# Zero products ahead of the first transposes, root norms by ScalarE, and one written order for VectorE's recurrent work

## The chip, the cores and the metric

The kernel runs on one core of one Trainium2 chip. A core has TensorE (PE in the profile; its weight loads are listed apart as PEld), VectorE (DVE), ScalarE (ACT), GpSimd (POOL) and SyncE (SP, which here only issues DMAs). The metric is the device time of one execution in microseconds, lower is better. The other numbers come from one further execution that the hardware profiler recorded.

## The reference

One layer of a hybrid decoder over 16 meta tokens and 1024 rows of width 1024, all in float32. `h` holds the meta rows and then the rows of `x`:

```python
u = rmsnorm(h, g_pre_mix)
z = u @ w_in                         # 1024 -> q 512 | k 128 | v 128 | xr 512 | yr 512
attn = sliding_window_attention_with_sinks(q, k, v, sinks)     # 8 heads of 64, window 128
xr = causal_depthwise_conv(xr, conv_w, conv_b)                 # 4 taps
hr = rg_lru(xr, ...)                 # gates by two block products, then h_t = a_t h_{t-1} + u_t
rec = gelu(yr) * hr
h = h + rmsnorm(concat(attn, rec) @ w_out, g_post_mix)
f = square(relu(rmsnorm(h, g_pre_ffn) @ w_ff1)) @ w_ff2        # 1024 -> 4096 -> 1024
h = h + rmsnorm(f, g_post_ffn)
```

`rmsnorm(x, g)` divides a row by the root of its mean square plus 1e-6 and multiplies by `g`. The gates use `mult = sqrt(1 - a*a)`.

## The kernel before

Each product is made of three: an operand is split into a high part (rounded to the type fp32r, by a cast) and a low part (what the cast left out), and high x high, high x low and low x high are summed in PSUM (`mm3`, L123; in block 0 `part`, L242, one of the three at a time over all eight slices of the depth, kc = 0 to 7). The high parts of weights and activations are made by ScalarE (L96, L117, L283), the low parts by VectorE (L99, L118, L287).

**Start.** SyncE's queue loads the meta rows, `x` rows 0 and 1 (each `xt[i]` is 128 rows x 1024), the two gain vectors, and then the column blocks of `w_in` for k, v, q and the first block of xr (`rk`, `rv`, `rq`, `rx`) with `xt[2]` to `xt[7]` between and after them. The rows are worked in four blocks (`ALL`, L251): block 0 holds the meta rows, `xt[0]` and `xt[1]`, and each later block two more `xt`. For a block, `norm_rows` (L212) makes the sum of squares on ScalarE (L215), adds EPS and takes the power -0.5 on GpSimd (`rstd_of`, L164: L167 and L173), and scales the rows on VectorE (L221). `transposed` (L289) then transposes them on TensorE (L296) slice by slice into PSUM and splits each slice into `u[kc]` high (ScalarE, L117) and low (VectorE, L118). The banks of PSUM in which the slices land have three tags with two buffers each (`pt`, `o`, `s`), so in block 0 six slices are under way before one must be emptied by both engines. In block 0, `chained` (L276) writes out an order for ScalarE (index 0) and VectorE (index 1): high part of the k weights, eight splits, then the v weights, the norms of `xt[2]` and `xt[3]`, the q weights and the xr weights. Products follow: k and v high, then their low weights, then q, then xr (L416 to L430).

**Middle.** Scores, softmax and attention of head pair j go on while `next_fill` (L674) projects the other column blocks (q, xr and yr) in between. The xr blocks are evicted from PSUM by ScalarE (`new_x`, L400, L404) and convolved by VectorE (`conv`, L618): a first tap with the bias over 1040 columns (L620) and three more (L625).

**Recurrent part.** `gates` (L729) makes two tanh gates for each of four 128-wide channel blocks c. `recur` (L770) takes a root on ScalarE and then, on VectorE, a scaling (L773), a product (L774) and the scan over time (L775). `rec_out` (L777) applies GeLU to one half (512 rows) of block c, multiplies (L781) and splits the result into `at`. In between, the row blocks kc of `w_out` are loaded by SyncE and split (`split_wo`, L794). The output products `out_mm` (L837) of row tile t run over kc = 0 to 7: kc 0 to 3 use the attention, kc 4 to 7 the recurrent blocks c = 0 to 3 together with `w_out` blocks 4 to 7. The first four tiles begin with kc 0 to 3, then take kc 4 and 5, then 6 and 7.

**Order.** Except where `behind` (L106) adds an ordering, which costs no semaphore, each engine's order is fixed when the kernel is built, by a planner that simulates the program. The functions below stand with the line numbers of the profile.

Of the kernel before, what the change touches and what calls it, by code (L numbers as in the profile page):

```python
# [9 lines left out]
F32 = mybir.dt.float32  # L10
F32R = mybir.dt.float32r
AF = mybir.ActivationFunctionType
ALU = mybir.AluOpType
# [24 lines left out]
def hybrid_layer(  # L38
# [42 lines left out]
    def lut(*args, **kwargs):  # L81
        ins = nc.scalar.activation(*args, **kwargs).ins
        if last_lut[0] is not None:
            tc.add_manual_dep(
                ins, last_lut[0],
                mybir.DependencyInfo(
                    mybir.DependencyClass.NoSync, mybir.DependencyReason.DATA
                ),
                reason="lut",
            )  # L90
        last_lut[0] = ins.name
        return ins

    def split(hi, lo, src, eng=None):
        if eng is None:
            nc.scalar.copy(hi, src)  # L96
        else:
            eng.tensor_copy(hi, src)
        low = nc.vector.tensor_tensor(lo, src, f32(hi), op=ALU.subtract).ins  # L99
        mark[0] = low.name  # L100
        return low
# [38 lines left out]
    meta_t = slot("d", [NMETA, D])  # L140
    nc.sync.dma_start(meta_t, meta_tokens)
    xt = []
# [5 lines left out]

    load_x(0)
    load_x(1)  # L150
    g_r = slot("e", [16, P])
    nc.sync.dma_start(g_r[0:8, :], g_pre_mix.rearrange("o (k p) -> (o k) p", p=P))
    nc.sync.dma_start(g_r[8:16, :], g_pre_ffn.rearrange("o (k p) -> (o k) p", p=P))

# [26 lines left out]
    held_back = []  # L181
# [28 lines left out]
    RMS_SC = 1.0 / math.sqrt(D)  # L210

    def norm_rows(src, n, link=False):  # L212
        xn = slot("d", [P, D])
        ssq = small.tile([P, 1], F32, name="ssq", tag="ssq")
        ins = nc.scalar.activation(  # L215
            xn[:n], src, AF.Square, scale=RMS_SC, accum_out=ssq[:n]
        ).ins
        if link:
            chained(0, ins)
        rs = rstd_of([ssq[:n]], n)  # L220
        ins = nc.vector.tensor_scalar(xn[:n], src, rs, None, op0=ALU.mult).ins  # L221
# [39 lines left out]
    vmt = const.tile([P, P], F32, name="vmt")  # L261
    nc.gpsimd.memset(f32(km), 0.0)
# [18 lines left out]
    def high_w(raw, tag="ws"):  # L281
        hi, lo = pair(tag, [P, KC, P])
        chained(0, nc.scalar.copy(hi, raw).ins)  # L283
        return hi, lo

    def low_w(w, raw):
        chained(1, nc.vector.tensor_tensor(w[1], raw, f32(w[0]), op=ALU.subtract).ins)  # L287

    def transposed(b, xn, after=None):  # L289
        t0, n = ALL[b]  # L290
        for kc in range(KC):
            flip[0] += 1
            pt = bank(("pt", "o", "s")[flip[0] % (2 if b == 1 else 3)])
            o = 0
            for s, m in xn:
                ins = nc.tensor.transpose(  # L296
                    pt[:, o : o + m], s[:m, kc * P : (kc + 1) * P], ident[:m, :m]
                )
# [46 lines left out]
    low_w(wx, rx)  # L345
# [51 lines left out]

        return q, sink_q

    def new_x(tag="d"):  # L400
        xr = slot(tag, [P, TT])

        def sink_x(acc, t0, n):
            nc.scalar.copy(xr[:, t0 : t0 + n], acc)  # L404

        return xr, sink_x


    done = [None, None]
    q0, sink_q0 = new_q()  # L410
    xr0, sink_x0 = new_x("c")
    for b in range(4):
        if b:
            transposed(b, xn if b == 1 else normed(b), done[b])
# [200 lines left out]

    xc = [None] * NLRU

    def conv(c, xr, tag="d"):  # L618
        y = slot(tag, [P, TT])
        taps = [nc.vector.tensor_scalar(  # L620
            y, xr, prm[:, c, 3:4], prm[:, c, 4:5], op0=ALU.mult, op1=ALU.add
        ).ins]
        for k in (2, 1, 0):
            s = 3 - k
            taps.append(nc.vector.scalar_tensor_tensor(  # L625
                y[:, s:], xr[:, : TT - s], prm[:, c, k : k + 1], y[:, s:],
                op0=ALU.mult, op1=ALU.add,
            ).ins)
        xc[c] = y
        if c == 2:  # L630
            held_back.extend(taps[4:])

    ys = [None] * NLRU
    begun = {}
# [7 lines left out]

    def fill_x(c):
        def run(w):
            xr, sink = new_x()
            project(w, ALL, sink)
            conv(c, xr, "b" if c == 3 else "d")
        return run

    def fill_y(c):  # L650
# [119 lines left out]
    def recur(c):  # L770
        r, gi, a = rg[c]
        lut(r, r, AF.Sqrt, scale=-0.25)
        nc.vector.scalar_tensor_tensor(r, a, 1.0, r, op0=ALU.add, op1=ALU.mult)  # L773
        nc.vector.tensor_tensor(gi, gi, r, op=ALU.mult)  # L774
        nc.vector.tensor_tensor_scan(r, a, gi, 0.0, op0=ALU.mult, op1=ALU.add)  # L775

    def rec_out(c, half):  # L777
        o = 512 * half
        y, h = ys[c][:, o : o + 512], rg[c][0]
        lut(y, y, AF.Gelu_apprx_tanh)  # L780
        nc.vector.tensor_tensor(y, y, h[:, NMETA + o : NMETA + o + 512], op=ALU.mult)  # L781
        ah, al = at[half][2 + c // 2]
        split(ah[:, c % 2, :], al[:, c % 2, :], y)
# [9 lines left out]

    def split_wo(kc, tag, eng=None):  # L794
        wo[kc] = pair(tag, [P, D])
        split(wo[kc][0], wo[kc][1], wo_raw[kc], eng)

    gate_parts(0)
    gate_parts(1)
# [6 lines left out]
    decay(3)  # L806
    next_fill()
    for c in range(NLRU):
        recur(c)
# [6 lines left out]
    for kc in range(2, 4):  # L816
        split_wo(kc, "a")
    for cp in (2, 3):
        at[0][cp] = pair("b", [P, 2, 512])
    for c in range(NLRU):  # L820
        rec_out(c, 0)
    for kc in range(4, KC):
        load_wo(kc, ("d", "raw")[kc % 2])
        split_wo(kc, "a")
# [589 lines left out]
```

## Time and profile before

| | |
|---|---|
| median of three runs | 959.78 us (958.34 to 960.52) |
| profiled execution, its own time | 961.63 us |
| its span, first to last instruction | 959.9 us (1.7 us lie around it) |
| granted TensorE clock, mean | 0.996 |
| busy: PE, PEld, DVE, ACT, POOL | 940.3, 784.9, 680.1, 495.0, 157.8 us |

In rows of a timeline the first number is the start in us from the span's start, the second the duration, then engine, line, operation, output and inputs, shapes, and the count; in square brackets stands how long the engine had been idle and what ended that. In rows of stretches each engine has its busy time and, in brackets, its instructions. In rows of waits stand the total in us, the number of waits and the longest.

### The profile page before, as it was taken

How to read it: one execution, taken by the hardware profiler on the slowest of the kernel's cores; microseconds unless marked ns; L12 is line 12 of the kernel's file. 1: busy time of each engine (PE TensorE's matmuls, PEld its weight loads, DVE VectorE, ACT ScalarE, POOL GpSimd, SP SyncE). 2: the span in 40 equal slices, each digit the busy share in tenths (PEclk: the TensorE clock that was granted, in tenths of full speed). 3: DMA queues.
4: the chain of work that ended last, by engine and by line, in shares of the span. 5: the costliest groups of instructions: out<-in, count | busy, mean ns of one | idle time of the engine just before them, and what ended most of it. 6: DMA issues, size and time to landing. Idle time of an engine off the chain costs nothing.

```text
span 959.9 us, 12395 instructions
## 1 busy us (share of the span) xinstructions
PE 940.3 (98%) x4654; PEld 784.9 (82%) x4654; DVE 680.1 (71%) x961; ACT 495.0 (52%) x818; POOL 157.8 (16%) x201
## 2 busy tenths in 40 slices
PE   6999999999999999999999999999999999999997
PEld 6999998878788877888888888888878888888886
DVE  5579989878966786665655466576557676779884
ACT  7556676468445464443555575663533344435451
POOL 4015656600021100000111001100111100003020
PEclk9999999999999999999999999999999999999999
DMA  9211101202236457585646557644767866566422
GB/s 286 53 48 42 38 8 34 66 21 90 88 132 219 131 180 237 157 282 175 219 165 209 154 182 231 219 135 132 170 148 186 199 219 197 178 193 156 113 85 88
DMA packets 85627, 140.74 MB, mean 147 GB/s; under 512 B 5784, under 2 KB 48936, under 8 KB 85568
## 3 DMA queue, kind: packets, MB, share of 16 engines
q1 hardware_dynamic: 75104, 108.51, 36.0%
q0 software_dynamic: 9600, 29.36, 11.9%
q10 hardware_dynamic: 864, 2.10, 0.6%
q8 instruction: 36, 0.59, 0.3%
q14 instruction: 23, 0.19, 0.1%
HBM read 115.70 MB, written 23.07 MB: 145 GB/s over the span
## 4 chain that ended last, share of the span: by engine, by line
PE 88%; DVE 6%; issue 2%; ACT 1%; POOL 1%; DMA 1%; DVEq 0%; SPq 0%; ACTq 0%; POOLq 0%
PE ps_acc L125 10%; PE ps_acc L128 10%; PE ps_acc L129 10%; PE ps_pt L129 6%; PE ps_s L129 6%; PE ps_pt L125 6%; PE ps_pt L128 6%; PE ps_s L128 6%; PE ps_s L125 6%; PE ps_o L129 5%; PE ps_o L128 5%; PE ps_o L125 5%; PE ps_o L597 1%; DVE c L775 1%; POOL c L587 1%
## 5 line engine op out<-in xcount | busy, mean ns | idle before, releaser
L96 ACT CAST ws<-raw 128x1024 fp32r<-128x1024 f32 (+1 forms) x70 | 71.7, 1025 | 120.8 <-PE ps_o L128 45.1
L99 DVE TENSOR_TENSOR ws<-raw,ws 128x1024 fp32r<-128x1024 f32 (+1 forms) x71 | 86.2, 1214 | 43.7 <-ACT ws L96 43.6
L125 PE MATMUL ps_acc<-a,ws 128*128 128x256 f32 (+2 forms) x256 | 85.9, 336 | 1.6 <-ACT d L404 1.4
L129 PE MATMUL ps_acc<-a,ws 128*128 128x256 f32 (+2 forms) x256 | 85.1, 333 | 0.0
L128 PE MATMUL ps_acc<-a,ws 128*128 128x256 f32 (+2 forms) x256 | 85.0, 332 | 0.0
L99 DVE TENSOR_TENSOR b<-b,b 128x1024 fp32r<-128x1024 f32 (+2 forms) x48 | 57.6, 1200 | 23.6 <-PE ps_o L128 15.3
L96 ACT CAST ws<-e 128x1024 fp32r<-128x1024 f32 x42 | 43.9, 1045 | 57.3 <-PE ps_o L128 34.7
L96 ACT CAST b<-b 128x1024 fp32r<-128x1024 f32 (+2 forms) x48 | 49.4, 1030 | 41.3 <-DVE b L912 40.5
L99 DVE TENSOR_TENSOR ws<-e,ws 128x1024 fp32r<-128x1024 f32 x42 | 51.4, 1223 | 20.0 <-ACT ws L96 20.0
L587 POOL TENSOR_SCALAR_AFFINE_SELECT c<-c 128x512 fp32r<-128x512 f32 x64 | 56.4, 905 | 26.3 <-ACT c L96 15.5
L173 POOL TENSOR_TENSOR rs<-ms,half_pow 128x1 f32<-128x1 f32 (+1 forms) x29 | 21.3, 740 | 207.6 <-DVE ms L169 206.2
L125 PEld LDWEIGHTS ps_acc<-a,ws 128*128 128x128 f32 x256 | 48.3, 189 | 6.8 <-ACT d L404 1.6
L129 PEld LDWEIGHTS ps_acc<-a,ws 128*128 128x128 f32 x256 | 48.2, 188 | 5.2 <-issue 0.2
L128 PEld LDWEIGHTS ps_acc<-a,ws 128*128 128x128 f32 x256 | 48.2, 188 | 4.5 <-issue 0.4
L128 PE MATMUL ps_acc<-ws,b 128*128 128x512 f32 (+1 forms) x120 | 46.6, 389 | 1.8 <-DVE ws L99 1.8
L129 PE MATMUL ps_acc<-ws,b 128*128 128x512 f32 (+1 forms) x120 | 46.6, 388 | 0.0
L125 PE MATMUL ps_acc<-ws,b 128*128 128x512 f32 (+1 forms) x120 | 46.4, 387 | 0.0
L125 PE MATMUL ps_pt<-ws,b 128*128 128x512 f32 x112 | 44.2, 395 | 0.0
L128 PE MATMUL ps_pt<-ws,b 128*128 128x512 f32 x112 | 44.1, 394 | 0.0
L129 PE MATMUL ps_pt<-ws,b 128*128 128x512 f32 x112 | 43.9, 392 | 0.0
L128 PE MATMUL ps_s<-ws,b 128*128 128x512 f32 x110 | 43.8, 398 | 0.0
L125 PE MATMUL ps_s<-ws,b 128*128 128x512 f32 x110 | 43.7, 397 | 0.0
(417 smaller groups left out, 2712.4 us busy)
## 6 DMA issues: line engine op xcount, KB each, us to landing
raw<-in_w_ff_dram SPq DMA_DIRECT2D x58, 512.0 KB, 4.4
e<-in_w_ff_dram SPq DMA_DIRECT2D x42, 512.0 KB, 4.2
raw<-in_w_in_dram SPq DMA_DIRECT2D x12, 512.0 KB, 5.7
d<-in_w_ff_dram SPq DMA_DIRECT2D x12, 512.0 KB, 4.1
s_dram<-d POOLq DMA_DIRECT2D x12, 512.0 KB, 4.0
e<-in_w_ff_dram POOLq DMA_DIRECT2D x10, 512.0 KB, 5.7
raw<-in_w_ff_dram POOLq DMA_DIRECT2D x10, 512.0 KB, 5.6
c<-in_x_dram SPq DMA_DIRECT2D x8, 512.0 KB, 8.2
```

The source lines that it names most:

```text
L96: nc.scalar.copy(hi, src)
L99: low = nc.vector.tensor_tensor(lo, src, f32(hi), op=ALU.subtract).ins
L125: ins = nc.tensor.matmul(dst, lh, rh, start=start, stop=False, skip_group_check=True).ins
L128: nc.tensor.matmul(dst, lh, rl, start=False, stop=False, skip_group_check=True)
L129: last_mm[0] = nc.tensor.matmul(dst, ll, rh, start=False, stop=stop, skip_group_check=True).ins.name
L173: last_pow[0] = nc.gpsimd.tensor_tensor(rs[:n], ms[:n], half_pow[:n], op=ALU.pow).ins.name
L587: nc.gpsimd.affine_select(out=m[:, :, side, :], in_=f32(m)[:, :, 1, :], pattern=[[0, 4], [-sign, P]], compare_op=op, fill=0.0, base=0, cha ...
L597: nc.tensor.matmul(po[:, :, oc : oc + n], v, m[:, :, pc : pc + n], start=first and k == 0, stop=last and k == 1, skip_group_check=True,)
L775: nc.vector.tensor_tensor_scan(r, a, gi, 0.0, op0=ALU.mult, op1=ALU.add)
```

## The change

Five things, all ahead of the feed-forward part; what is computed stays the same.

1. **Products of zeros.** TensorE multiplies `km`, just set to zero, with itself into a bank that nobody reads: 11 products of 512 columns as soon as `km` is set, 4 more (`waiting`) behind the transpose of `xt[0]`'s slice 4, and one of 256 columns behind the last transpose of each of the eight slices of block 0. That bank is one of the two of tag `acc`.
2. **Norms of block 0** (`norm_first`): ScalarE takes the root of mean square plus EPS itself and VectorE the reciprocal; GpSimd is left out. For `xt[0]` the sum of squares is shared, 576 columns by ScalarE and 448 by VectorE. The scaling of `xt[0]` and `xt[1]` is made in two halves of 512 columns. The first table that ScalarE loads is the root's.
3. **Weights at the start.** The high part of the k weights is cast by VectorE in place of ScalarE; the cast of the q weights moves ahead of the norms of `xt[2]` and `xt[3]`. The gains land in `vmt`, no longer in a buffer of tag `e`.
4. **Convolution of block c = 2:** the first tap is made by ScalarE from PSUM, piece by piece, right after the copy.
5. **Recurrent part:** the pieces of `recur`, `rec_out` and `split_wo` that VectorE runs get one written order (`queue`); GeLU runs once over 1024 columns per block, no longer twice over 512.

```diff
-    g_r = slot("e", [16, P])
+    vmt = const.tile([P, P], F32, name="vmt")
+    g_r = vmt[:16, :]
...
+    eps_t = const.tile([P, 1], F32, name="eps_t")
+    nc.gpsimd.memset(eps_t, EPS)
+    root = small.tile([P, 1], F32, name="root", tag="root")
+    lut(root, half_pow, AF.Sqrt, scale=-1.0)
...
+    ROW_HALVES = (slice(0, 512), slice(512, D))
+    def norm_first(src, n, cut, parts):
+        xn = slot("d", [P, D])
+        ssq = small.tile([P, 1], F32, name="ssq", tag="ssq")
+        nc.scalar.activation(
+            xn[:n, :cut], src[:n, :cut], AF.Square, scale=RMS_SC, accum_out=ssq[:n]
+        )
+        rest = eps_t
+        if cut < D:
+            rest = small.tile([P, 1], F32, name="ms", tag="ms")
+            nc.vector.tensor_tensor_reduce(
+                out=xn[:, cut:], in0=src[:, cut:], in1=src[:, cut:], scale=1.0 / D,
+                scalar=EPS, op0=ALU.mult, op1=ALU.add, accum_out=rest,
+            )
+        root = small.tile([P, 1], F32, name="root", tag="root")
+        lut(root[:n], ssq[:n], AF.Sqrt, bias=rest[:n])
+        rs = small.tile([P, 1], F32, name="rs", tag="rs")
+        nc.vector.reciprocal(rs[:n], root[:n])
+        for c in parts:
+            chained(1, nc.vector.tensor_scalar(
+                xn[:n, c], src[:n, c], rs[:n], None, op0=ALU.mult
+            ).ins)
+        return xn
...
+    idle, still = bank("acc"), km.rearrange("p a b c -> p (a b c)")
+    def idling(n, cols=512, after=None):
+        made = []
+        for _ in range(n):
+            ins = nc.tensor.matmul(
+                idle[:, :cols], still[:, :P], still[:, :cols],
+                start=True, stop=True, skip_group_check=True,
+            ).ins
+            if after:
+                behind(after, ins)
+            made.append(ins)
+        return made
+    idling(11)
+    waiting = idling(4)
...
     def normed(b):
-        rows = [(meta_t, NMETA)] if b == 0 else []
-        rows += [(xt[2 * b], P), (xt[2 * b + 1], P)]
-        return [(norm_rows(s[:m], m), m) for s, m in rows]
+        if b == 0:
+            return [
+                (norm_first(meta_t, NMETA, D, (slice(0, D),)), NMETA),
+                (norm_first(xt[0], P, 576, ROW_HALVES), P),
+                (norm_first(xt[1], P, D, ROW_HALVES), P),
+            ]
+        return [(norm_rows(xt[i], P), P) for i in (2 * b, 2 * b + 1)]
...
+                if b == 0 and o == NMETA and kc == 4:
+                    behind(ins.ins.name, *waiting)
                 o += m
+            if b == 0:
+                idling(1, 256, ins.ins.name)
...
-    wk = high_w(rk, "b")
+    wk = high_w(rk, "b", 1)
     transposed(0, xn)
     low_w(wk, rk)
     wv = high_w(rv, "b")
     low_w(wv, rv)
+    wq = high_w(rq)
     xn = [(norm_rows(xt[i], P, True), P) for i in (2, 3)]
-    wq = high_w(rq)
...
         def sink_x(acc, t0, n):
             nc.scalar.copy(xr[:, t0 : t0 + n], acc)
+            if y is not None:
+                nc.scalar.activation(
+                    y[:, t0 : t0 + n], acc, AF.Identity,
+                    scale=prm[:, c, 3:4], bias=prm[:, c, 4:5],
+                )
...
+    lane = []
+    def queue(ins):
+        if lane:
+            behind(lane[-1].name, ins)
+        lane.append(ins)
...
     for c in range(NLRU):
-        rec_out(c, 0)
-    for kc in range(4, KC):
+        lut(ys[c], ys[c], AF.Gelu_apprx_tanh)
+    queue(input_scale(0))
+    queue(input_gate(0))
+    queue(split_wo(3, "a"))
+    queue(scan(0))
+    for kc in (4, 5):
         load_wo(kc, ("d", "raw")[kc % 2])
-        split_wo(kc, "a")
+    queue(rec_mult(0, 0))
+    queue(input_scale(1))
+    queue(input_gate(1))
+    queue(scan(1))
+    queue(rec_low(0, 0))
+    queue(rec_mult(1, 0))
+    queue(split_wo(4, "a"))
+    queue(rec_low(1, 0))
+    queue(split_wo(5, "a"))
+    queue(input_scale(2))
+    for kc in (6, 7):
+        load_wo(kc, ("d", "raw")[kc % 2])
+    queue(input_gate(2))
+    queue(scan(2))
+    queue(rec_mult(2, 0))
+    queue(input_scale(3))
+    queue(rec_low(2, 0))
+    queue(input_gate(3))
+    queue(scan(3))
+    queue(rec_mult(3, 0))
+    queue(split_wo(6, "a"))
+    queue(rec_low(3, 0))
+    queue(split_wo(7, "a"))
     for cp in (2, 3):
         at[1][cp] = pair("b", [P, 2, 512])
     for c in range(NLRU):
-        rec_out(c, 1)
+        queue(rec_mult(c, 1))
+    for c in range(NLRU):
+        queue(rec_low(c, 1))
```

`input_scale`, `input_gate`, `scan`, `rec_mult` and `rec_low` are the instructions of L773, L774, L775, L781 and of the split at L783, each in a function of its own.

More of the change, by code (lines that the diff above doesn't have):

```diff
@@ L279, in chained, with high_w @@
         last[e] = ins.name
-    def high_w(raw, tag="ws"):
+    def high_w(raw, tag="ws", e=0):
         hi, lo = pair(tag, [P, KC, P])
-        chained(0, nc.scalar.copy(hi, raw).ins)
+        cast = (nc.scalar.copy, nc.vector.tensor_copy)[e]
+        chained(e, cast(hi, raw).ins)
         return hi, lo
@@ L398, in new_q, with new_x @@
         return q, sink_q
-    def new_x(tag="d"):
+    def new_x(tag="d", c=0):
         xr = slot(tag, [P, TT])
+        y = slot("d", [P, TT]) if c == 2 else None
         def sink_x(acc, t0, n):
             nc.scalar.copy(xr[:, t0 : t0 + n], acc)
-        return xr, sink_x
+            if y is not None:
[3 more added lines that the diff above has]
+                )
+        return xr, sink_x, y
     done = [None, None]
     q0, sink_q0 = new_q()
-    xr0, sink_x0 = new_x("c")
+    xr0, sink_x0, _ = new_x("c")
     for b in range(4):
@@ L616, in hybrid_layer, with conv @@
     xc = [None] * NLRU
[L618 to L622, printed above, removed]
+    def conv(c, xr, tag="d", y=None):
+        if y is None:
+            y = slot(tag, [P, TT])
+            nc.vector.tensor_scalar(
+                y, xr, prm[:, c, 3:4], prm[:, c, 4:5], op0=ALU.mult, op1=ALU.add
+            )
         for k in (2, 1, 0):
             s = 3 - k
-            taps.append(nc.vector.scalar_tensor_tensor(
+            nc.vector.scalar_tensor_tensor(
                 y[:, s:], xr[:, : TT - s], prm[:, c, k : k + 1], y[:, s:],
                 op0=ALU.mult, op1=ALU.add,
-            ).ins)
+            )
         xc[c] = y
-        if c == 2:
-            held_back.extend(taps[4:])
     ys = [None] * NLRU
@@ L644, in run @@
         def run(w):
-            xr, sink = new_x()
+            xr, sink, y = new_x(c=c)
             project(w, ALL, sink)
-            conv(c, xr, "b" if c == 3 else "d")
+            conv(c, xr, "b" if c == 3 else "d", y)
         return run
@@ L768, in decay, with root, input_scale, input_gate @@
         lut(v, v, AF.Tanh, scale=m2sp[:, c : c + 1], bias=m2sp[:, c : c + 1])
-    def recur(c):
-        r, gi, a = rg[c]
[L772 to L777, printed above, removed]
+    lane = []
[3 more added lines that the diff above has]
+        lane.append(ins)
+    def root(c):
+        lut(rg[c][0], rg[c][0], AF.Sqrt, scale=-0.25)
+    def input_scale(c):
+        r, gi, a = rg[c]
+        return nc.vector.scalar_tensor_tensor(
+            r, a, 1.0, r, op0=ALU.add, op1=ALU.mult
+        ).ins
+    def input_gate(c):
+        r, gi, a = rg[c]
+        return nc.vector.tensor_tensor(gi, gi, r, op=ALU.mult).ins
+    def scan(c):
+        r, gi, a = rg[c]
+        return nc.vector.tensor_tensor_scan(
+            r, a, gi, 0.0, op0=ALU.mult, op1=ALU.add
+        ).ins
+    def rec_mult(c, half):
         o = 512 * half
         y, h = ys[c][:, o : o + 512], rg[c][0]
-        lut(y, y, AF.Gelu_apprx_tanh)
-        nc.vector.tensor_tensor(y, y, h[:, NMETA + o : NMETA + o + 512], op=ALU.mult)
+        return nc.vector.tensor_tensor(
+            y, y, h[:, NMETA + o : NMETA + o + 512], op=ALU.mult
+        ).ins
+    def rec_low(c, half):
         ah, al = at[half][2 + c // 2]
-        split(ah[:, c % 2, :], al[:, c % 2, :], y)
+        y = ys[c][:, 512 * half : 512 * half + 512]
+        return split(ah[:, c % 2, :], al[:, c % 2, :], y)
     wo_raw = [None] * KC
@@ L795, in split_wo @@
         wo[kc] = pair(tag, [P, D])
-        split(wo[kc][0], wo[kc][1], wo_raw[kc], eng)
+        return split(wo[kc][0], wo[kc][1], wo_raw[kc], eng)
     gate_parts(0)
@@ L808, in hybrid_layer @@
     for c in range(NLRU):
-        recur(c)
+        root(c)
     load_wo(0, "raw")
@@ L815, in hybrid_layer @@
     split_wo(1, "e")
-    for kc in range(2, 4):
-        split_wo(kc, "a")
+    split_wo(2, "a")
     for cp in (2, 3):
```

2 lines of the change are left out of this document (removed).

## The prediction

> **What bounds the kernel now.** First the page's busy times and the chain that ended last, then the stretches, then the list of TensorE's waits.
>
> ```profile
> PE 940.3 (98%) x4654; PEld 784.9 (82%) x4654; DVE 680.1 (71%) x961; ACT 495.0 (52%) x818; POOL 157.8 (16%) x201
> PE 88%; DVE 6%; issue 2%; ACT 1%; POOL 1%; DMA 1%; DVEq 0%; SPq 0%; ACTq 0%; POOLq 0%
> ...
> 5.80:13.50 7.70, 6.04 (x27) 4.94 (x28) 3.94 (x9) 5.88 (x12) 1.78 (x4) 1.00 1.10 316
> 50.00:80.00 30.00, 30.00 (x216) 27.97 (x215) 23.38 (x79) 15.28 (x44) 8.45 (x7) 1.00 0.20 54
> 150.00:176.00 26.00, 24.60 (x183) 23.16 (x182) 22.93 (x55) 17.26 (x48) 17.77 (x16) 1.00 0.13 35
> 245.00:262.00 17.00, 15.99 (x69) 12.40 (x68) 17.00 (x17) 5.33 (x8) 0.00 (x0) 1.00 0.26 82
> ...
> PE ps_s L296 <- DVE d L221: 5.8, 1, 5.8
> PE ps_acc L125 <- ACT d L404: 1.4, 1, 1.4
> PE ps_pt L129 <- DVE b L99: 1.0, 2, 0.5
> ```
>
> TensorE is busy 98% of the span and carries 88% of the chain. What the edited parts can give is therefore only what TensorE loses there: the start, one wait of 1.4 us on ScalarE's copy of an xr block (the idle part of the stretch 150 to 176), and two waits of 1.0 us together on VectorE's low parts of the recurrent blocks (245 to 262, where VectorE is busy 17.00 of 17.00 us). After that TensorE runs on through code that isn't edited.
>
> **The start, step by step.** The timeline of the first 26 us, every engine, then the answer on the `x` tiles:
>
> ```profile
> 0.97 0.52 POOL L262 MEMSET km<- 128x512 f32 x1
> 6.80 1.06 ACT L215 ACTIVATE d<-c 128x1024 f32<-128x1024 f32 x1 [0.18 <-DMA c<-in_x_dram]
> 7.39 2.56 SPq L146 DMA_DIRECT2D c<-in_x_dram  x3
> 8.54 0.57 POOL L173 TENSOR_TENSOR rs<-ms,half_pow 128x1 f32<-128x1 f32 x1
> 8.70 0.42 PE L296 MATMUL ps_s<-ident,d 128*128 128x128 f32 x1
> 8.91 0.42 PE L296 MATMUL ps_pt<-ident,d 128*128 128x128 f32 x1
> 9.14 0.75 DVE L221 TENSOR_SCALAR d<-c,rs 128x1024 f32<-128x1024 f32 x1 [0.69 <-POOL rs L173]
> 9.22 1.05 ACT L283 CAST b<-raw 128x1024 fp32r<-128x1024 f32 x1 [1.27 <-DMA raw<-in_w_in_dram]
> 10.63 0.49 ACT L117 ACTIVATE a<-ps_o,gcol 128x272 fp32r<-128x272 f32 x1 [0.36 <-PE ps_o L296]
> 13.83 0.49 ACT L117 ACTIVATE a<-ps_s,gcol 128x272 fp32r<-128x272 f32 x1 [0.33 <-PE ps_s L296]
> 14.22 1.04 ACT L283 CAST b<-raw 128x1024 fp32r<-128x1024 f32 x1
> 19.40 0.75 DVE L221 TENSOR_SCALAR d<-c,rs 128x1024 f32<-128x1024 f32 x1 [0.77 <-POOL rs L173]
> 19.70 0.27 PE L296 MATMUL ps_pt<-ident,d 128*128 128x128 f32 x1
> 19.80 0.27 PE L296 MATMUL ps_o<-ident,d 128*128 128x128 f32 x1
> 19.94 2.15 PE L245 MATMUL ps_s<-a,ws 128*128 128x256 f32 x16
> 20.07 1.22 DVE L287 TENSOR_TENSOR ws<-e,ws 128x1024 fp32r<-128x1024 f32 x1
> 20.17 0.16 ACT L360 CAST km<-ps_acc 64x16 fp32r<-64x16 f32 x1
> 22.28 4.21 PE L245 MATMUL ps_s<-a,ws 128*128 128x256 f32 x32
> ...
> DMA to landing us min/median/max: 7.8/8.2/8.6
> ```
>
> The rows of `xt[1]` land just before 6.80 in both kernels; ScalarE's square sum ends near 8.0. Before, GpSimd's add and power follow, VectorE scales from 9.14 to 9.89, and ScalarE begins the eight splits at 10.63. Now follow a root on ScalarE and a reciprocal on VectorE over one column. Neither is in this part of the trace; each costs between the 0.16 us of the smallest row above and the 0.57 of GpSimd's power. I take 0.2, as these engines' small rows lie there. Half a scaling is 0.4 (of 0.75). So the first half stands at 8.0 + 0.4 + 0.4 = 8.8, and after one transpose of 0.42 the splits begin near 9.25. The shared sum over `xt[0]` gains about as much, a step earlier, and is not the last to arrive.
>
> The k cast on VectorE waits for the landing at 9.2 and takes less than ScalarE's 1.05; it ends before the first low split can begin, which costs nothing.
>
> The splits come 0.37 to 0.40 us apart (before: eight in 10.63 to 13.83 with one break at the last, for a bank). Eight from 9.25 put the v cast at 12.3 in place of 14.22: 1.9 us earlier. Behind that cast the same 32 products of k and v stand, so TensorE reaches the q products near 18.0 in place of 19.94 and ends their first 16 (2.15 us) near 20.2.
>
> There the gain meets another bound. The low q weights (20.07 + 1.22 = 21.29) stand on VectorE behind the norm of `xt[3]`, which this change leaves with GpSimd. `xt[2]` is issued from 7.39 and lands not before 15.2 (with the shortest landing, 7.8), so that norm and the 21.29 don't move. If TensorE keeps the order of before, the 32 products of 22.28 start at 21.3: **1.0 us** gained. If the planner puts the xr products ahead, all 1.9 remain. I take **1.4**, the middle, as no row tells the order; the bounds are 0.5 (a late bank or clock as below) and 2.2.
>
> The products of zeros start after 1.5 us. 32 products of about 260 columns take 4.21 us, so one of 512 is about 0.26 us at full pace and 0.52 at half; the two pairs of transposes show the two paces, 0.21 apart at 8.7 and 0.10 at 19.7 (PEclk reads 1.00 in both). Eleven end between 4.4 and 7.3 us, while TensorE would wait 5.8 us for the first rows; `xt[0]`'s first half comes near 7.1. What is hidden there costs 0.2 at most. The four `waiting` (1.0 to 2.1 us) lie in the hole between the two `xt`, and the eight of 256 columns (0.13 to 0.26 each) beside splits 0.37 apart; uncovered and at half pace they would cost 8 x 0.26 = 2.1. For all of these I add nothing.
>
> [...]
>
> ScalarE's first table is now the root's, so one more table load comes at the first exponential. It falls into the stretch 50 to 80, where ScalarE is busy 15 of 30 us and TensorE all 30; without that cover it would cost the 1.28 us of the load quoted below. The gains in `vmt`, GpSimd's later memset of it, and a buffer `e` that is free earlier add nothing: neither GpSimd nor that DMA is waited for there.
>
> **The convolution.** From the timelines of VectorE and ScalarE:
>
> ```profile
> 147.27 1.12 DVE L620 TENSOR_SCALAR d<-d,prm 128x1040 f32<-128x1040 f32 x1
> ...
> 157.08 0.36 ACT L610 COPY e<-ps_o 64x256 f32<-64x256 f32 x1 [0.98 <-DVE e L611]
> 157.47 0.39 ACT L404 COPY d<-ps_acc 128x272 f32<-128x272 f32 x1
> ```
>
> The copy that TensorE waits for stands on ScalarE behind one that waited for VectorE, and VectorE works almost without a break from 147 on. Its first tap (1.12, of which 0.07 overlaps) goes away, so the copy comes about **1.0 us** earlier of the 1.4. The bounds are 0 (VectorE's next wait takes its place) and 1.4. ScalarE gets four pieces of 0.37 to 0.49 (rows of L404 and L117), 1.5 to 2.0 us, some ten us earlier; they hold a bank of `acc` that much longer. TensorE needs over 2 us for a piece (24 products at 0.13) and has a second bank, so this is hidden; uncovered it costs those 2.0.
>
> **The recurrent part.** VectorE, ScalarE and TensorE:
>
> ```profile
> 232.84 2.40 DVE L773 SCALAR_TENSOR_TENSOR c<-b,c 128x1040 f32<-128x1040 f32 x2 [1.72 <-ACT c L82]
> 236.66 1.28 ACT L82 ACT_TABLE_LOAD   x1
> 239.74 2.32 DVE L775 TENSOR_TENSOR_SCAN c<-b,c 128x1040 f32<-128x1040 f32 x1
> 246.50 1.27 DVE L781 TENSOR_TENSOR d<-d,c 128x512 f32<-128x512 f32 x2
> 247.68 1.22 DVE L99 TENSOR_TENSOR a<-d,a 128x1024 fp32r<-128x1024 f32 x1
> 255.26 0.50 PE L129 MATMUL ps_pt<-a,b 128*128 128x512 f32 x1 [0.54 <-DVE b L99]
> 261.56 0.72 PE L129 MATMUL ps_pt<-a,b 128*128 128x512 f32 x2 [0.47 <-DVE b L99]
> 263.50 0.39 PE L125 MATMUL ps_pt<-a,b 128*128 128x512 f32 x1
> ```
>
> No work is added, only its order changes; less an overlap of 0.08, scalings and products step by 1.15, scans by 2.24, multiplications and low parts of 512 columns by 0.6, low weights by 1.13. Summed in the written order from 232.84: up to the low weights of kc 5, four scalings and products 4.6, two scans 4.5, four short ones 2.4, three weights 3.4, so 247.7. TensorE waited for these at 255.26 and 261.56: both waits go, **1.0 us**. The next need is kc 6 and 7, at 263.50 before and 262.5 without the waits. The order reaches the last of them after another 4.6 + 4.5 + 2.4 + 2.3 = 13.8, at 261.5, with half a microsecond or so lost to casts at 262.0. So late next are the weights of kc 7, by a margin of 0.5. Bounds: a loss of the whole 1.0 if that margin is overrun, to 1.3 (starts, not idle time). The long GeLU has the same elements; the first ends about 1.2 us after the table load, near 239.1, when the order reaches it at 238.5 to 239.
>
> **The sum.** 1.4 + 1.0 + 1.0 = 3.4 us off the profiled execution's 961.63, so 958.2 for such an execution; the runs' median stands 1.85 below it, and 959.78 - 3.4 = **956.4**. All of it assumes that what follows shifts with TensorE, since the other engines are fed by it.
>
> **Rivals.** First, only the start gains: the planner rebuilds the middle and other waits come in place of the two, as VectorE's 17.00 of 17.00 speaks for; 959.78 - 1.4 = 958.4. Second, only the two later waits go, since the unchanged 21.29 and the order take all of the start; 957.8. Third, the clock closes again after the zeros: `xt[1]`'s six slices at 0.21 + 0.26 in place of 0.37 cost 0.6, and two us of products at half pace 1.0; q's 16 products then end at 21.8, the start gains 0.5, and the time is 957.3. [...]
>
> Fourth, slower: VectorE stalls in the written order. Whatever it waits for in the lane (a GeLU, a cast, a late block of `w_out`) now holds all that stands behind, one to one beyond the margin of 0.5: 956.4 + W - 0.5. It is no gain from W = 3.9 and 962 at W = 6. For it speaks that VectorE has no idle time there, against it that ScalarE is busy 5.33 of 17 us and the inputs counted above are there in time. Fifth, slower: the zeros keep TensorE at half pace, past 13.2 us where products ran at full pace before. Each us more costs 0.5; it eats the later 2.0 at 17 us, and at 22 us the time is 962.2. No row shows zeros at all; that real products reached full pace within some 2 us speaks against it.
>
> **How the numbers follow.** Forecast 0.52, first 0.12, second 0.10, third 0.11, fourth 0.09, fifth 0.06. A measurement of this kernel tells about 0.2% (1.9 us, so 957.9 and 961.7) from no change. Faster: 0.52 + 0.11 and half of the second, 0.68; within 0.2%: the first and half of the second, 0.17; slower 0.15. Low end: 2.2 + 1.4 + 1.3 gives 954.9, and 1.0 for a planner's luck elsewhere 953.9. High end 960.3: it holds the first three rivals and some overrun of the fourth.
>
> **What would show it.** Right: ScalarE's first L117 split near 9.3 and the v cast near 12.3; transposes 0.10 apart by 9 us; q's products begun near 18; no wait of TensorE near 157 on the copy, none on low parts of kc 4 and 5; VectorE without idle time from the first scaling to the last low part. Wrong: the q products begun later than before, a wait of TensorE for kc 6 or 7 over 1 us, or new waits on ScalarE between 50 and 150.

## The result and the profile after

| | before | after |
|---|---|---|
| median of six runs each | 959.8 us (958.07 to 961.54) | 955.66 us (955.25 to 957.34) |
| ratio | 1 | 0.9964, 95% interval 0.9952 to 0.9976 |
| span of the profiled execution | 959.9 us | 953.5 us |

The forecast was 956.4. The ratio makes the change 3.5 us faster (2.3 to 4.6) where 3.4 was forecast; the two medians differ by 4.1. The two profiled executions differ by more, 6.4 us; why is told below.

After, the list of TensorE's waits, and the stretches (busy us and count of PE, PEld, DVE, ACT, POOL):

```profile
PE ps_acc L298 <- POOL km L292: 1.6, 1, 1.6
PE ps_acc L125 <- ACT d L460: 1.0, 1, 1.0
PE ps_o L658 <- POOL c L648: 0.9, 1, 0.9
...
5.80:13.50 7.70, 7.15 (x49) 5.64 (x49) 6.45 (x19) 5.84 (x15) 0.20 (x1) 1.00 1.08 359
150.00:176.00 26.00, 25.05 (x182) 23.45 (x181) 22.01 (x53) 16.23 (x48) 15.11 (x17) 1.00 0.18 50
176.00:190.00 14.00, 13.09 (x64) 10.63 (x63) 12.22 (x18) 6.61 (x12) 5.47 (x5) 1.00 0.23 69
245.00:262.00 17.00, 16.94 (x74) 13.38 (x72) 16.83 (x16) 3.57 (x5) 0.00 (x0) 1.00 0.20 58
```

The 5.8 us before the first rows are now a wait of 1.6 for the zeros' operand. The two waits on low parts (L129) are gone, and the stretch 245 to 262 is full. The wait near 157 has shrunk from 1.4 to 1.0, and the one on GpSimd that ends at 184.35 has grown to 0.9; before it was 0.2.

The start after, from the timeline (ScalarE, VectorE, TensorE):

```profile
6.54 1.06 ACT L237 ACTIVATE d<-c 128x1024 f32<-128x1024 f32 x1 [0.22 <-DMA c<-in_x_dram]
7.32 0.27 PE L347 MATMUL ps_s<-ident,d 128*128 128x128 f32 x1
7.43 0.27 PE L347 MATMUL ps_pt<-ident,d 128*128 128x128 f32 x1
7.72 0.29 ACT L82 ACTIVATE root<-ssq,eps_t 128x1 f32<-128x1 f32 x1
8.05 0.16 DVE L250 RECIPROCAL rs<-root 128x1 f32<-128x1 f32 x1 [0.56 <-ACT root L82]
9.13 0.68 DVE L334 CAST b<-raw 128x1024 fp32r<-128x1024 f32 x1
9.31 0.49 ACT L117 ACTIVATE a<-ps_o,gcol 128x272 fp32r<-128x272 f32 x1 [1.29 <-DVE gcol L159]
12.46 0.49 ACT L117 ACTIVATE a<-ps_s,gcol 128x272 fp32r<-128x272 f32 x1 [0.28 <-PE ps_s L347]
12.85 1.04 ACT L334 CAST b<-raw 128x1024 fp32r<-128x1024 f32 x1
14.74 1.05 ACT L220 ACTIVATE d<-c 128x1024 f32<-128x1024 f32 x1
19.07 1.22 DVE L338 TENSOR_TENSOR ws<-e,ws 128x1024 fp32r<-128x1024 f32 x1
```

Root and reciprocal take 0.29 and 0.16; the first split begins at 9.31 in place of 10.63, the last at 12.46 in place of 13.83. What the first split waited for last is VectorE's copy of the gains (`gcol`, L159, at 9.05), which stands behind the second half of the scaling. The transposes step by 0.11 at 7.4 us, where they stepped by 0.21 before. Below, the clock is called open where TensorE steps at the faster of these two paces, and half where it steps at the slower.

**Where the time went.** The same TensorE instructions were found in each trace: the first transpose of the parameters (near 53 us, behind the start), the first gate product (near 197, behind the middle) and the first transpose of an output tile (near 285, behind the recurrent part). All are starts in us.

| kernel | first, eighth split | parameters | first gate | output tile | middle | recurrent |
|---|---|---|---|---|---|---|
| before | 10.63, 13.83 | 53.48 | 197.77 | 285.65 | 144.29 | 87.88 |
| e1, before again | 10.74, 14.19 | 53.84 | 198.15 | 286.73 | 144.31 | 88.58 |
| after | 9.31, 12.46 | 52.11 | 196.49 | 283.25 | 144.38 | 86.76 |
| f3, after again | 9.22, 12.38 | 52.01 | 196.42 | 283.13 | 144.41 | 86.71 |
| e2, start only | 9.80, 12.97 | 52.59 | 196.85 | 284.40 | 144.26 | 87.55 |
| e3, tap only | 10.76, 14.20 | 53.85 | 198.38 | 286.34 | 144.53 | 87.96 |
| e4, order only | 10.57, 13.78 | 53.44 | 197.76 | 284.86 | 144.32 | 87.10 |
| e5, no zeros | 9.60, 12.21 | 51.88 | 196.31 | 283.19 | 144.43 | 86.88 |
| e6, zeros only | 11.39, 14.89 | 54.57 | 198.86 | 287.01 | 144.29 | 88.15 |
| e7, no tap | 9.66, 12.81 | 52.46 | 196.72 | 283.42 | 144.26 | 86.70 |
| e8, taps 2 and 3 | 10.60, 14.32 | 53.98 | 198.17 | 285.46 | 144.19 | 87.29 |
| f1, norms and order | 9.36, 12.80 | 52.50 | 196.72 | 283.18 | 144.22 | 86.46 |
| f2, more zeros | 10.06, 12.85 | 52.49 | 196.71 | 283.53 | 144.22 | 86.82 |
| f4, k cast on ScalarE | 10.61, 14.15 | 53.77 | 197.99 | 284.95 | 144.22 | 86.96 |

The last two columns are differences of neighbours. From before to after the parameters come 1.37 us earlier, the gates 1.28, the output tile 2.40: start +1.37, middle -0.09, recurrent +1.12. That is 2.4 us of the span's 6.4. Nearly all of the rest arises near 700 us, where no line was edited: there the lead over before, by the starts of the same products, grows from 2.4 to 6.0. The profile of before there, VectorE and TensorE, then three stretches:

```profile
698.82 1.23 DVE L912 TENSOR_TENSOR e<-e,raw 128x1024 f32<-128x1024 f32 x1 [7.02 <-DMA raw<-in_w_ff_dram]
702.37 0.50 PE L128 MATMUL ps_acc<-ws,b 128*128 128x512 f32 x1 [1.79 <-DVE ws L99]
...
697.00:702.00 5.00, 3.58 (x16) 2.59 (x14) 3.18 (x3) 0.73 (x1) 0.00 (x0) 1.00 0.17 38
702.90:706.20 3.30, 3.30 (x9) 2.52 (x9) 2.94 (x3) 1.41 (x2) 1.21 (x1) 0.50 0.52 163
706.30:710.00 3.70, 3.70 (x17) 3.01 (x17) 1.29 (x2) 1.05 (x1) 0.00 (x0) 1.00 1.01 218
```

A load of feed-forward weights came late, VectorE waited 7 us for it and TensorE 1.8; the clock then fell to 0.50 for 3.4 us: 9 products start in 3.3 us of it, where 17 do in 3.7 us afterwards. Together that is the 3.6 us by which the lead grows.

### The profile page after: what moved, and what is told of

Read it like the earlier page. It is cut to its first block, busy times and chain, and to the rows that moved or that the text cites. A ratio compares the mean times of both kernels' runs of the same rounds, so it can differ in the third digit from the quotient of the medians.

```text
span 953.5 us, 12448 instructions
## 1 busy us (share of the span) xinstructions
PE 942.0 (99%) x4677; PEld 785.7 (82%) x4677; DVE 682.4 (72%) x968; ACT 498.3 (52%) x822; POOL 152.7 (16%) x196
## 4 chain that ended last, share of the span: by engine, by line
PE 88%; DVE 7%; ACT 2%; issue 1%; DMA 1%; POOL 1%; DVEq 0%; SPq 0%; ACTq 0%; POOLq 0%
PE ps_acc L125 10%; PE ps_acc L128 10%; PE ps_acc L129 10%; PE ps_pt L128 6%; PE ps_pt L129 6%; PE ps_pt L125 6%; PE ps_s L125 6%; PE ps_s L129 6%; PE ps_s L128 6%; PE ps_o L125 5%; PE ps_o L128 5%; PE ps_o L129 5%; DVE c L852 1%; PE ps_o L658 1%; PE ps_o L996 1%
## 5 line engine op out<-in xcount | busy, mean ns | idle before, releaser
L99 DVE TENSOR_TENSOR ws<-raw,ws 128x1024 fp32r<-128x1024 f32 (+1 forms) x71 | 85.4, 1203 | 45.5 <-ACT ws L96 45.5
L129 PE MATMUL ps_acc<-a,ws 128*128 128x256 f32 (+2 forms) x256 | 85.0, 333 | 0.0
L99 DVE TENSOR_TENSOR b<-b,b 128x1024 fp32r<-128x1024 f32 (+2 forms) x48 | 57.6, 1199 | 25.5 <-PE ps_o L128 19.8
L99 DVE TENSOR_TENSOR ws<-e,ws 128x1024 fp32r<-128x1024 f32 x42 | 51.3, 1222 | 20.0 <-ACT ws L96 20.0
L129 PEld LDWEIGHTS ps_acc<-a,ws 128*128 128x128 f32 x256 | 48.2, 188 | 5.1 <-issue 0.2
L178 POOL TENSOR_TENSOR rs<-ms,half_pow 128x1 f32<-128x1 f32 x26 | 19.3, 749 | 205.9 <-DVE ms L174 204.7
L129 PE MATMUL ps_acc<-ws,b 128*128 128x512 f32 (+1 forms) x120 | 46.2, 385 | 0.0
L129 PE MATMUL ps_pt<-ws,b 128*128 128x512 f32 x112 | 43.9, 392 | 0.0
L129 PE MATMUL ps_s<-ws,b 128*128 128x512 f32 x110 | 43.2, 393 | 0.0
```

The costliest lines, as they stand in the source:

```text
L129: last_mm[0] = nc.tensor.matmul(dst, ll, rh, start=False, stop=stop, skip_group_check=True).ins.name
L178: last_pow[0] = nc.gpsimd.tensor_tensor(rs[:n], ms[:n], half_pow[:n], op=ALU.pow).ins.name
```

## The experiments

Medians and ratios are against before on the same chip, five rounds each. A ratio of before with itself came out at 1.0009 (e1), so about 1 us is what such a ratio can tell.

**e1: before, unchanged.**

> The unchanged kernel once more. In the profiled execution of before, TensorE loses 3.7 us near 700 us (a wait of 1.8 us on a low part of w_ff weights whose load landed late, then some 5 us at half pace), which no edited line touches. Theory A: that is an accident of one execution; a second profile shows no such wait, a span some 2 to 4 us under 959.9, and the ratio of times is 1.000 within 0.0015. Theory B: the old order of instructions causes it, so it stands in this profile too.

Median 959.39, ratio 1.0009 (1.0000 to 1.0018), span 958.2. TensorE has no wait at all between 680 and 720, so theory A holds for this further profile. The event isn't alone in its kind, though: TensorE waits for late feed-forward weights in other profiles too, for 0.64 us up to 763.19 in e1, 1.29 up to 763.16 in e3, 0.72 up to 760.42 in e5 and 0.32 up to 699.16 in e7. Only in the first profile of before did the clock fall behind it (half clock stood there for 3.4 us, not the 5 named above). The recurrent part cost 0.7 more here than in the first profile (88.58 against 87.88), so single profiles scatter by that much.

**e2: start only.** The changed kernel with parts 4 and 5 undone.

```diff
-    queue(input_scale(0))
...
+    for c in range(NLRU):
+        recur(c)
...
-        y = slot("d", [P, TT]) if c == 2 else None
```

> Before with parts 1 to 3 alone (zeros, block 0's norms, weights at the start). The same products of TensorE stand 1.37 us earlier from 13 us on in the changed kernel. Theory: that lead is all of the start's, so 1.4 us faster, ratio 0.9985, and the lead stays 1.4 to the end. Rival: the later waits (157, 255, 261) grow by what the start gained, and the time is that of before.

Median 957.08, ratio 0.9985 (0.9976 to 0.9994): 1.4 us. The parameters come 0.9 us before those of before and 1.25 before e1's, and the middle keeps it. The start's gain isn't eaten.

**e3: tap only.** Before with `new_x`, `conv` and `fill_x` of the changed kernel.

> Before with part 4 alone (first tap of block c = 2 by ScalarE). Theory from the traces: the wait of 1.4 near 157 shrinks by some 0.4 and a later one on GpSimd near 184 appears, so 0 +- 0.3 us, ratio 1.000. Rival, the prediction: 1.0 us faster, ratio 0.999.

Median 959.26, ratio 1.0007 (0.9998 to 1.0015). The list of waits of e3, TensorE:

```profile
PE ps_acc L125 <- ACT d L405: 1.0, 1, 1.0
PE ps_o L603 <- POOL c L593: 0.9, 1, 0.9
```

Against 1.4 and 0.2 in before these are 1.0 and 0.9. The middle takes 144.53 us in place of 144.29 to 144.31: the tap costs 0.2.

**e4: order only.** Before with the functions and the queue of part 5.

> Before with part 5 alone (one written order of VectorE's recurrent work). Theory: both waits on the low parts of kc 4 and 5 go and nothing takes their place, TensorE's lead rises by 1.1 near 262, ratio 0.9989. Rival: without the earlier start the order overruns its margin at kc 7, and less than 0.5 us is left.

Median 957.68, ratio 0.9992 (0.9983 to 1.0001), by the median 1.0 us; the interval holds 1, so the times alone don't show the gain. The recurrent part takes 87.10 in place of 87.88 and 88.58. Its only wait of TensorE between 225 and 285 is

```profile
PE ps_pt L128 <- DVE a L99: 0.4, 1, 0.4
```

a low part of `w_out` weights in a high x low product: the margin at kc 6 and 7 was overrun by 0.4, as the rival says, and 0.8 to 1.5 is left. The table is firmer than this pair: the nine profiles with the written order take 86.46 to 87.29 us there, the five without it 87.55 to 88.58, on the mean 1.2 more. And e7 is e2 with this order and nothing else; its ratio is 0.9970 where that of e2 is 0.9985.

**e5: no zeros.** The changed kernel with `idle`, `idling` and `waiting` taken out.

> The changed kernel without its 23 products of zeros. Theory: the zeros bring TensorE to full pace at 5 us; without them the transposes step by 0.21 again, the first split comes some 0.3 us later and the last some 0.5 later, so the start's lead of 1.37 falls to about 0.7 and the time rises by 0.7 us against the changed kernel (2.7 us under before). Rival: the norms alone make the start, the lead stays 1.2 to 1.4, and the zeros are worth nothing.

Median 956.91, ratio 0.9978 (0.9967 to 0.9989). In its profile the start is the best of all, parameters at 51.88. Transposes step by 0.21 up to 10.2 and full pace comes at 10.65, yet the eight splits follow within 2.61 us (9.60 to 12.21), where the changed kernel takes 3.15 (9.31 to 12.46). In this execution the theory falls. The times lean its way (0.9978 against 0.9964 and 0.9969 for the changed kernel), but the intervals overlap.

**e6: zeros only.** Before with the zeros alone.

```diff
+    idling(11)
+    waiting = idling(4)
...
+            if b == 0:
+                idling(1, 256, ins.ins.name)
```

> Before with part 1 alone. Theory: the clock opens at 5 us, transposes step by 0.10, but GpSimd's norms still set the first split at 10.2 to 10.6 us; lead 0.3 to 0.6 us from 14 us on, ratio 0.9995. Rival: the zeros stand in front of real products and cost up to 0.5 us.

Median 959.88, ratio 1.0023 (1.0010 to 1.0035), slower. Stretches of its start, where the last but two numbers are the clock:

```profile
5.90:9.20 3.30, 1.91 (x14) 1.37 (x13) 1.02 (x3) 2.02 (x5) 1.74 (x4) 1.00 1.09 295
9.30:12.60 3.30, 3.30 (x14) 2.63 (x13) 1.16 (x3) 1.89 (x4) 0.00 (x0) 0.50 1.14 336
```

The clock opened at 5.9 and fell back to half at 9.3. The four `waiting` zeros begin at 8.72, and the next transpose starts only at 10.10; the zeros behind the later transposes then run at a clock of 0.50 in front of the next. First split 11.39, 0.7 later than before's.

**e7: no tap.** The changed kernel with the tap of c = 2 back on VectorE.

> The changed kernel with the first tap of c = 2 back on VectorE. Theory: the lead over before at 190 us stays near 1.3 and the time is that of the changed kernel within 0.3 us. Rival: the wait near 157 is 1.4 again and the time rises by 0.5 to 1.0.

Median 956.43, ratio 0.9970 (0.9959 to 0.9980). The wait near 157 is 1.4 again, that on GpSimd is 0.2 as in before, and the middle is 144.26 in place of 144.38 and 144.41. The tap costs 0.1 in the trace, which the times can't tell.

**e8: taps of c = 2 and 3.**

```diff
-        y = slot("d", [P, TT]) if c == 2 else None
+        y = slot("d" if c == 2 else "b", [P, TT]) if c > 1 else None
```

> The changed kernel with the first tap of block c = 3 by ScalarE as well. VectorE makes that tap from 171.3 to 172.4, ahead of the low part that GpSimd's selects at 173.7 wait for, and these end in TensorE's wait of 0.9 us near 184. Theory: that wait shrinks by the tap's 1.1, so the time falls by 0.7 to 0.9 against the changed kernel. Rival: the casts of ScalarE (170 to 173) come later by the four new pieces, and the wait stays.

Median 955.87, ratio 0.9979 (0.9968 to 0.9989). The wait on GpSimd is gone, as expected. The one near 157 is 1.4, and it now ends on ScalarE's tap of c = 3 (0.58 us), which stands behind the copy and holds the same bank. The middle is 144.19, 0.2 better than after; without any tap by ScalarE it takes 144.22 to 144.32, so nothing is gained that can be told. The start of this profile is another matter:

```profile
4.70:8.00 3.30, 2.02 (x14) 1.40 (x13) 2.50 (x7) 2.12 (x5) 0.20 (x1) 1.00 0.96 320
8.10:11.40 3.30, 3.30 (x13) 2.82 (x13) 2.01 (x6) 1.10 (x3) 0.00 (x0) 0.50 1.10 336
11.60:15.00 3.40, 3.40 (x25) 2.68 (x24) 2.75 (x8) 2.64 (x7) 0.00 (x0) 1.00 1.04 370
```

Up to the splits its code is that of the changed kernel, and its parameters come at 53.98, 1.9 us later, of which 0.4 is a later landing of `xt[1]`. The clock was open from 4.7, half from 8.1 to 11.5. What that costs first is the four `waiting` zeros, here and then in the changed kernel:

```profile
8.08 2.06 PE L298 MATMUL ps_acc<-km 128*128 128x512 f32 x4
9.93 0.42 PE L347 MATMUL ps_pt<-ident,d 128*128 128x128 f32 x1
...
7.63 1.17 PE L298 MATMUL ps_acc<-km 128*128 128x512 f32 x4
8.64 0.27 PE L347 MATMUL ps_pt<-ident,d 128*128 128x128 f32 x1
```

This is the third rival, in one execution. That execution took 957.9 us, 2.0 above the kernel's median.

**f1: norms and order.** The changed kernel without zeros and without the tap.

> The changed kernel without the zeros and without the tap by ScalarE: norms, weights at the start and the written order alone. Theory: these two make all of the gain, so TensorE leads before by 1.3 to 1.9 us from 17 us on and by 3 to 3.5 after 270, and the median is within 0.5 us of the changed kernel's, 3 us under before. Rival: without zeros the real products meet a half-rate clock in most executions and the median is 1 us over the changed kernel's.

Median 955.46 (five runs), ratio 0.9968 (0.9956 to 0.9979). Here full pace came only at 13.1 us and the last split stood at 12.80; the output tile comes at 283.18, as in the changed kernel. It is e7 without the zeros, and the two ratios are 0.9968 and 0.9970. Norms, weights at the start and the order thus make all of the gain that can be told.

**f2: more zeros.**

```diff
-    idling(11)
-    waiting = idling(4)
+    idling(15)
+    waiting = idling(6)
...
-            if b == 0:
+            if b == 0 and kc < 6:
```

> The changed kernel without the tap, with 15 zero products at first, 6 behind xt[0]'s slice 4, and of the eight of 256 columns only six (none behind slices 6 and 7). In one look of eight the clock fell back to half between 8.1 and 11.5 us and the splits came 1.3 us later. [...] Rival: zeros beyond what the hole holds delay the transposes, and the lead falls under 1.2.

Median 956.37, ratio 0.9976 (0.9966 to 0.9986). More zeros were to hold the clock open and to bring the first split by 9.7 and the last by 12.4. The clock stayed open in this profile, with TensorE busy 3.40 of 3.40 us from 5.36 on, but the longer row of zeros delays the transposes: first split 10.06, last 12.85. No better than fewer zeros or none.

**f3: after again.**

> The changed kernel once more, beside the others: 955.7 to 956.3 us, ratio 0.9970. Its profile shows whether the clock stays open from 5 us (lead 1.4 to 1.7 at 17 us) or falls back (lead near 0).

Median 955.28, ratio 0.9969 (0.9958 to 0.9981). The clock opened at 6.5 and stayed; its three columns repeat after's within 0.1.

**f4: k cast on ScalarE.** The changed kernel without the tap, and

```diff
-    wk = high_w(rk, "b", 1)
+    wk = high_w(rk, "b")
```

> The changed kernel without the tap and with the cast of the k weights back on ScalarE. The weights land at 8.3 to 9.2, so ScalarE casts until about 10.2 and the first split moves from 9.3 to 10.2, the last from 12.5 to about 13.1. Theory: the lead falls by 0.6 to 0.7 and the time rises by as much. Rival: the low parts begin sooner on VectorE, the last slice no longer waits for a bank, and nothing is lost.

Median 955.74, ratio 0.9970 (0.9960 to 0.9981): no loss that the times can tell (e7, with the cast on VectorE, has 0.9970 as well). Its profile can't judge the cast, since TensorE ran at half pace up to 11.1 us. ScalarE cast from 9.23 to 10.28, then waited 0.33 for a slow transpose and began at 10.61.

## Why the prediction was right, and where it wasn't

**The sum** was right by its number: 3.4 forecast, 3.5 by the ratio. The terms don't add up to it. By the means of the table's profiles the recurrent part gives 1.2 and the tap -0.2, and the start gives 1.2 as counted below: together 2.2, and 2.4 in the profiled pair. That is just under and just inside the ratio's 2.3 to 4.6, so a term of 1.0 that gave nothing was covered by the scatter, which is luck. Where a further microsecond might come from stays open; the late loads of feed-forward weights differ from execution to execution and cost 3.6 us in before and 0.9 in e1, where after had none.

**The start**, 1.4 forecast and 1.37 measured, was right through errors that cancel, so by luck too. The rows of `xt[1]` land at a time of their own in each execution: ScalarE's sum over them starts at 6.38 to 7.03 us, and in after 0.26 earlier than in before. From there to the v cast the kernels take:

| profiles | clock | us |
|---|---|---|
| before, e1, e3, e4 | half until 13.3 to 14.7 | 7.42 to 7.66 |
| after, f3, e2, e7 | full from 5.1 to 6.5 | 6.31 to 6.33 |
| f2, more zeros first, none behind the last two slices | full from 5.4 | 6.56 |
| e5, no zeros | full from 10.65 | 5.79 |
| f1, no zeros | full from 13.1 | 6.77 |
| e8 | half from 8.1 to 11.5 | 7.76 |
| e6, zeros alone | half from 9.3 to 12.7 | 8.56 |
| f4, k cast on ScalarE | half until 11.1 | 8.16 |

The edits are thus worth 1.1 to 1.3 of the 1.37, and the rest is the earlier landing. The forecast's 6.80 to 12.3 is 5.5, 0.8 less than the changed kernel takes. The first split came where it was put (9.3) only because the rows came 0.26 early; from the sum it is 2.77, not 2.45, since the split waited for the copy of the gains. The v cast was put at 12.3 and came at 12.85. The step that failed there is "eight from 9.25": the break at the last split, which the forecast reads in before's rows, is left out of its sum without a reason, and it is still there (11.69 to 12.46). In before TensorE comes late with the last slices at half pace, in after with zeros in front of them, which were priced at nothing. Without zeros and at full pace (e5) there is no break and the splits take 2.61 us; without zeros at half pace (f1) they take 3.44, with zeros at full pace 3.15 to 3.17.

The other error is the bound that was to hold TensorE at 21.3. SyncE's queue issued `xt[2]` at 6.81 in place of 7.39, ScalarE could begin it at 14.74, and the low q weights were ready at 20.3, a microsecond sooner. Eight q products ran already from 17.25 and eight from 19.19, where 16 were forecast from 18. TensorE ran from 13 us on without a wait, and the lead is that of the eighth split, 13.83 - 12.46 = 1.37.

**The zeros.** That they would bring the faster pace was the author's estimate, as no row of before shows any. The clock opened behind them at 4.7 to 6.5 us in seven of the eight profiles that have them (in f4 at 11.1), and they are worth nothing that can be told. With them and an open clock (after, f3, e2, e7) the parameters come at 52.0 to 52.6, without zeros at 51.9 (e5) and 52.5 (f1), and where the clock fails (e8, f4) at 53.8 to 54.0. Two of seven profiles of kernels with these norms and zeros ran at half pace where it mattered, so the third rival was one of executions, not of kernels. It was priced at 0.9 us and cost 1.4 in e8, by the table; f4's 1.8 holds the k cast too. The price left out the four `waiting` zeros, which at half pace hold TensorE for 1.85 us in front of the slices of `xt[1]`.

**The tap** was wrong: 1.0 forecast, -0.1 to -0.2 measured (e3, e7, after). The step that failed is "the copy comes about 1.0 us earlier". VectorE and ScalarE after, then VectorE before; the copy of before stands in the forecast:

```profile
148.81 3.27 DVE L687 SCALAR_TENSOR_TENSOR d<-d,prm,d 128x1038 f32<-128x1038 f32 x2
152.93 1.22 DVE L99 TENSOR_TENSOR ws<-raw,ws 128x1024 fp32r<-128x1024 f32 x1
154.99 0.68 DVE L118 SCALAR_TENSOR_TENSOR b<-ps_acc,b 64x512 fp32r<-64x512 f32 x1
156.98 0.39 ACT L460 COPY d<-ps_acc 128x272 f32<-128x272 f32 x1
...
152.65 1.29 DVE L625 SCALAR_TENSOR_TENSOR d<-d,prm,d 128x1037 f32<-128x1037 f32 x1
154.78 0.68 DVE L118 SCALAR_TENSOR_TENSOR b<-ps_acc,b 64x512 fp32r<-64x512 f32 x1
155.49 1.23 DVE L99 TENSOR_TENSOR ws<-raw,ws 128x1024 fp32r<-128x1024 f32 x1
```

VectorE's last tap ends at 152.08 in place of 153.94. But the forecast took the order of all other work as it was, and the planner built another: low weights (L99) that stood behind the split L118 now stand ahead of it, with two more score maxima, so L118 comes no earlier, nor do the copies of ScalarE behind it. Counted from the parameters, the copy comes at 104.9 in after and 105.0 in e3, and at 104.0 in before and e7: the tap made it 0.9 to 1.0 us later. TensorE's wait shrank all the same, to 1.0, because other products now run ahead of it. At 184 the wait on GpSimd grew; VectorE's tap of c = 3 stands ahead of the low part that GpSimd needs, and in e8 that wait goes when that tap goes. The bound of 0 should have been the value, and the first rival ("the planner rebuilds the middle") is what happened here.

**The order** was right: 1.0 forecast, 1.12 between the profiles, 0.8 to 1.5 alone, 1.2 on the mean. The low parts of VectorE after, in the written order (weights of kc 3, of kc 4 and 5, then of kc 6, the recurrent block 3, the weights of kc 7), and the two products of TensorE around its need of the last:

```profile
234.40 1.23 DVE L99 TENSOR_TENSOR a<-raw,a 128x1024 fp32r<-128x1024 f32 x1 [0.34 <-ACT a L96]
244.54 1.22 DVE L99 TENSOR_TENSOR a<-d,a 128x1024 fp32r<-128x1024 f32 x1
246.28 1.22 DVE L99 TENSOR_TENSOR a<-raw,a 128x1024 fp32r<-128x1024 f32 x1
258.92 1.22 DVE L99 TENSOR_TENSOR a<-d,a 128x1024 fp32r<-128x1024 f32 x1
260.05 0.68 DVE L99 TENSOR_TENSOR b<-d,b 128x512 fp32r<-128x512 f32 x1
260.65 1.22 DVE L99 TENSOR_TENSOR a<-raw,a 128x1024 fp32r<-128x1024 f32 x1
...
261.47 0.39 PE L125 MATMUL ps_pt<-a,b 128*128 128x512 f32 x1
261.92 0.50 PE L128 MATMUL ps_pt<-a,b 128*128 128x512 f32 x1
```

It ends with kc 5 at 247.5 and with kc 7 at 261.9; forecast, less the 1.3 us by which the whole stretch stands earlier, were 246.4 and 260.2 to 260.7. The sum was thus 1.1 us short: scalings and products step by 1.27 to 1.28 where 1.15 was taken, and VectorE waits 0.34 for a cast at 234.4, so it was not without idle time. The margin of 0.5 was therefore mis-sized. Even in after TensorE's product at 261.92 starts 0.45 behind the one before it, where the others step by 0.23, just when the weights of kc 7 are ready (260.65 and 1.22); elsewhere it waits 0.2 (e5), 0.3 (f4), 0.4 (e4) and 0.6 (e8) for them. The forecast named the right next need, and the two waits went, which is why the gain holds. The fourth rival came as these tenths only.

**The profiled pair** overstates the change. Its own times are 961.63 and 955.25, and the event near 700 of the first then counts as a gain that no edit made.

The clock changed at 4.68, 8.09 and 11.50 us in e8 and at 5.86, 9.27 and 12.68 in e6, each time 3.41 us apart. In e5, which has no zeros, it opened at 10.65 behind transposes: in the 3.41 us before, TensorE was busy 3.14, and up to 10.28 it ran nothing but transposes, which the trace lists as matmuls:

```profile
7.24:10.65 3.41, 3.14 (x14) 2.88 (x15) 2.98 (x9) 2.03 (x6) 0.07 (x1) 1.00 1.14 351
...
7.79 0.45 PE L344 MATMUL ps_o<-ident,d 128*128 128x128 f32 x1 [0.20 <-DVE d L252]
10.21 0.42 PE L344 MATMUL ps_pt<-ident,d 128*128 128x128 f32 x1
10.28 0.68 PE L276 MATMUL ps_acc<-a,b 128*128 128x272 f32 x2
```

## What to carry to other kernels

Before a wait is counted as gained, ask whether the order of everything around it stays: the tap went, the planner put other work in its place, and the copy came 0.9 us later. The order's gain held because the order was written out and the next need in it had been looked up. Filler work that is to raise a clock must not stand in front of the work it is to speed up (in e8 four products of zeros held TensorE for 1.85 us at half clock), and whether it works differed between executions, at half pace in two of seven profiles here; judge it by many. And compare several profiles stage by stage by the starts of the same instruction: a whole span can hold an accident as large as the change (3.6 us here, and 3.5). Count a stage from the landing of its data, which moves by itself (here from 6.38 to 7.03 us): so counted, four profiles of the same start agree within 0.02 us.

## What the runs showed of the hardware

The zeros: products of 512 columns stepped by 0.43 us up to 5 us and by 0.23 afterwards (after), with nothing but zeros run until then.

A fall to half was read in three profiles. In the 3.4 us before, TensorE had been busy 2.01 us (e6, to 9.27), 2.12 (e8, to 8.09) and 1.61 (before, 699.4 to 702.8), and 3.4 us at half clock followed each time. In before those 3.4 us held a single wait of 1.8 us; behind the wait of 1.3 in e3 the clock did not fall. It stayed open while TensorE was busy, of 3.40 us, 2.22 (e2, from 5.12), 2.80 (e7, from 6.02), 2.85 (after, from 5.16), 3.28 (f3, from 6.46) and 3.40 (f2, from 5.36).

Ahead of an opening TensorE had been busy 3.10 of 3.40 us (e8, to 4.68) and 3.14 of 3.41 (e5, to 10.65). In f4 it was busy 2.68 of 3.40 us from 0.86 and was counted busy from 4.27 to 7.67 throughout, 2.2 us of it with zeros and the rest with transposes, mostly of 16 rows; yet the clock stayed at half up to 11.1, and why isn't known. All of these are single executions.

ScalarE's further table load stands at 59.92 us in after, ahead of the first exponential at 61.22, and takes 1.28 us; TensorE is busy throughout from 59.90 to 61.20.
